# Six of sixteen pairs of row tiles of an MLP's first product by seven half-size products in place of eight, with the sums on GpSimd

## The chip, the cores and the metric

One core of one Trainium2 chip runs the whole kernel. The metric is the device time of one execution in microseconds; the time before is the median of three runs, 869.11 us (869.0 to 869.13). The engines have short names in the rows: PE is TensorE (PEld its weight loads), DVE is VectorE, ACT is ScalarE, POOL is GpSimd, SP is SyncE, which issues the DMA transfers. Each engine works through its own instructions in a fixed order.

## The reference

The kernel computes one decoder block in float32 on 512 tokens of width 1024: two attention-like branches, merged, then a squared-ReLU MLP, then gated embeddings. The change lies in the MLP:

```
x = x + merged @ w_out
h = rms_norm(x, mlp_norm_g)
x = x + jnp.square(jax.nn.relu(h @ w_ff1)) @ w_ff2      # w_ff1: 1024 x 4096, w_ff2: 4096 x 1024
gate = jax.nn.sigmoid(rms_norm(x, ple_norm_g) @ w_ple_gate)
x = x + gate * (p @ w_ple_proj)
return rms_norm(x, final_norm_g)
```

## The kernel before

**Products in three parts.** A float32 operand is split into a high part (`w_hi`, a copy rounded to fp32r, by ScalarE, line 175) and a low part (`w_lo`, the difference, by VectorE, line 176). A product of two split operands is three matmuls: high by high, high by low, low by high. `mm3` (lines 186 to 194) issues them with a weight tile of 128x128 as the stationary operand and the activations as the moving one; `rows3` (lines 201 to 209) has the activations stationary and the weights moving. `split` (line 220) does the same for activations.

**Weights.** All weights come as units of 128x1024 in the fixed order of the list `seq`. `load_to` issues the load of a unit into `w_raw` (two buffers), `fetch_to` makes its `w_hi` and `w_lo` (three buffers each), and `weights` hands it to the product. `fetch_to` runs two units ahead of the product, so the `w_hi` of a unit waits until TensorE is done with the unit three before it.

**The MLP in quarters.** The 4096 hidden rows are done in four quarters (`for qd`, lines 1216 to 1245). In each, the first product makes eight tiles of 128 hidden rows by 512 tokens (`m` from 0 to 7), each from one weight unit: 8 x 3 = 24 matmuls of 512 columns into one PSUM bank. `squared` (lines 1148 to 1167) takes max(0, .) times the norm's scale (`rs2`) on VectorE, squares on ScalarE, and builds the operands of the second product.

The second product is already done by seven block products in place of eight (Strassen in Winograd's form): the hidden rows 0 to 3 and 4 to 7 of the quarter and the two halves of the tokens are the blocks on one side, four weight blocks B11, B12, B21, B22 on the other. `seventh(qd, i, ...)` is one of the seven, of two weight units (p_ = 0 and 1) and 24 matmuls; `LEFT` lists its activation operand (`fA11`, `fA2`, `fS`, `fS3`), `RIGHT` its weight operand. The weight blocks are loaded into eight tiles of their own by `load_block`; the sums of them (T2, T1, T4 and B12 - B22) are made by VectorE (`sums_early`, `T1`, `T4`). `to_x` adds a finished result from PSUM to the residual `xs`.

**Order.** A scheduler places the instructions of every engine by their readiness in its own model; the program text gives the dependences, and `issue_after` adds a few by hand. GpSimd has no work in the MLP. The SBUF space is nearly full.

Of the kernel before, what the change touches and what calls it, by code (L numbers as in the profile page):

```python
# [18 lines left out]
P = 128  # L19
T = 512  # L20
# [20 lines left out]
U_PLE, U_QKV, U_RW, U_GSB, U_GRW, U_UPSB, U_UPRW, U_OUT, U_FF1, U_FF2, U_GATE = range(11)  # L41
UNITS = {U_PLE: 2, U_QKV: 12, U_RW: 14, U_GSB: 8, U_GRW: 8, U_UPSB: 4, U_UPRW: 4, U_OUT: 8, U_FF1: 32, U_FF2: 32, U_GATE: 8}
# [5 lines left out]
NUNITS = _n  # L48

# [36 lines left out]
def tile_block(ctx: ExitStack, tc: tile.TileContext, xT, xt, pT, wts, lora, cols_d, gfin_d, consts_d, out, dbg=None):  # L86
# [60 lines left out]
    ready, loaded = {}, []  # L147
# [3 lines left out]
    sources = {}  # L151

    def unit(i):
        return wts[UBASE[seq[i][0]] + seq[i][1]]

    def load_to(n):
        while len(loaded) < min(n, len(seq)):
            i = len(loaded)
            loaded.append(None)
            if seq[i][0] != U_FF2:  # L160
                loaded[i] = wpool.tile([P, 1024], F32, name="w_raw", bufs=2)
                sync.dma_start(out=loaded[i], in_=unit(i))

    def fetch_to(n, ahead=0):
        while state["i"] < min(n, len(seq)):
            i = state["i"]
            state["i"] += 1
            load_to(i + 1 + ahead)
            raw = loaded[i] if seq[i][0] != U_FF2 else sources[seq[i]]()
            if seq[i] in homes:  # L170
                hi, lo = homes[seq[i]]()
            else:
                hi = wpool.tile([P, 1024], F32R, name="w_hi")
                lo = wpool.tile([P, 1024], F32R, name="w_lo")
            act.copy(out=hi, in_=raw)  # L175
            dve.tensor_tensor(out=lo, in0=raw, in1=r32(hi), op=ALU.subtract)  # L176
            ready.setdefault(seq[i], []).append((hi, lo))

# [7 lines left out]
    def mm3(ps, w, base, rhs, k, first, last, t=slice(0, T)):  # L186
# [4 lines left out]
        pe.matmul(ps, wh, xh[:, k, t], start=first, stop=False)  # L191
        pe.matmul(ps, wh, xl[:, k, t], start=False, stop=False)  # L192
        pe.matmul(ps, wl, xh[:, k, t], start=False, stop=last)  # L193
        step()
# [82 lines left out]
    with ExitStack() as sA:  # L277
# [43 lines left out]
        with ExitStack() as s1:  # L321
# [18 lines left out]
            raws = [wpool.tile([P, 1024], F32, name="w_raw", bufs=2) for _ in range(2)]  # L340
# [719 lines left out]
    def norm_of(pool_, name):  # L1060

        st = pool_.tile([P, 3, TT], F32, name=name)
        sq = pool_.tile([P, D], F32, name="sqj", tag="T2a")
# [43 lines left out]
    fA11, fS3 = ([p4.tile([P, 4, HT], F32R, name=f"{n}{i}") for i in range(2)] for n in ("fA11", "fS3"))  # L1107
# [6 lines left out]
    LEFT = (fA11, part(fA2, 0), part(fS, 1), part(fS, 0), fS3, part(fS, 2), part(fA2, 1))  # L1114
# [4 lines left out]
    def kept(tt):  # L1119
        t = p4.tile([P, 512], F32, name="pl", tag="rk", bufs=4)  # L1120
        return t
# [7 lines left out]
    r2 = norm_of(p4, "st2")  # L1129

    def spread():

        ps = ps_main()
        for tt in range(TT):
            dg = p4.tile([P, P], F32, name="dg", bufs=2)
            dve.tensor_scalar(out=dg, in0=ident, scalar1=r2[:, tt:tt + 1], scalar2=float(D), op0=ALU.mult, op1=ALU.mult)
            pe.matmul(ps[:, tt * P:(tt + 1) * P], onesd, dg, start=True, stop=True)
        act.copy(out=rs2, in_=ps)
# [7 lines left out]
    lower = {}  # L1146

    def squared(ps, m):
        if m < 4:
            r = lower[m] = p4.tile([P, T], F32, name="rk", bufs=4)  # L1150
        else:
            r = p4.tile([P, T], F32, name="r")
# [3 lines left out]
        lo_, hi_ = r[:, 0:HT], r[:, HT:T]  # L1156
        if m < 4:
            split(fA11[0][:, m], fA11[1][:, m], lo_)
            minus(sums[:, 0], lo_, hi_)
            split(fS3[0][:, m], fS3[1][:, m], sums[:, 0])  # L1160
        else:
            k, low = m - 4, lower[m - 4]
            split(fA2[0][:, k], fA2[1][:, k], r.rearrange("p (j t) -> p j t", j=2))
            plus(sums[:, 1], low[:, HT:T], hi_)
            minus(sums[:, 2], sums[:, 1], low[:, 0:HT])
            minus(sums[:, 3], lo_, sums[:, 2])
            split(fS[0][:, k], fS[1][:, k], sums[:, 1:4])
# [3 lines left out]
    def load_block(qd, n, p_):  # L1171

        i = {"B11": 0, "B21": 2, "B12": 4, "B22": 6}[n] + p_
        t = blocks[n, p_] = p4.tile([P, 1024], F32, name=f"{n}{'ab'[p_]}")
        sync.dma_start(out=t, in_=wts[UBASE[U_FF2] + qd * 8 + i])

    def sums_early(p_):

        minus(blocks["B12", p_], blocks["B22", p_], blocks["B12", p_])
        blocks["T2", p_] = p4.tile([P, 1024], F32, name=f"T2{'ab'[p_]}")  # L1180
        plus(blocks["T2", p_], blocks["B12", p_], blocks["B11", p_])

    def T1(p_):
        minus(blocks["B11", p_], blocks["B22", p_], blocks["T2", p_])

    def T4(p_):
        minus(blocks["B21", p_], blocks["B21", p_], blocks["T2", p_])

    RIGHT = ("B11", "B21", "T2", "B11", "B12", "B22", "B21")
    BEFORE = {4: lambda: T1(0), 5: lambda: T1(1), 7: lambda: T4(0), 8: lambda: T4(1)}  # L1190
    for qd in range(4):
        for i in range(7):
            for p_ in range(2):
                def source(i=i, p_=p_):
                    BEFORE.get(2 * i + p_, lambda: None)()
                    return blocks[RIGHT[i], p_]
                sources[U_FF2, qd, i, p_] = source
    LOADS = [[("B12", 0), ("B22", 0)], [("B11", 0), ("B12", 1)], [("B22", 1), ("B11", 1)], [("B21", 0), ("B21", 1)]]
# [16 lines left out]

    for qd in range(4):
        waiting = []
        for m in range(8):
            w = weights(U_FF1, qd * 8 + m)
            for l in LOADS[m] if m < 4 else ():  # L1220
                load_block(qd, l[0], l[1])
            ps = ps_main()
            product(ps, w, hx)
            waiting.append((ps, m))
            if qd == 0 and m < 2:
                continue
            if qd == 0 and m == 2:
                spread()
            while waiting:
                squared(*waiting.pop(0))  # L1230
            if m in (2, 4):
                sums_early(m // 2 - 1)
# [12 lines left out]
        to_x(V, 1, 0)  # L1245

# [179 lines left out]
```

## Time and profile before

| what | value |
|---|---|
| median of the runs | 869.11 us |
| the profiled execution | 869.75 us, of which its span 867.7 us |
| granted TensorE clock, mean | 0.998 |
| everything ahead of the MLP's first product | 0 to about 480 us |
| the MLP's four quarters | 480 to 806.9 us |
| embeddings, gate, final norm, output | 806.9 to 867.7 us |

The second, third and fourth quarter start at 562.07, 643.67 and 725.27 us (the first matmul of each), and each takes 81.6 us. In the rows that follow, a line of a group gives line, engine, operation, output and inputs by the names of the program, shapes and count, then busy time and the mean of one in ns, then the idle time just ahead of them and who ended it. A line of a timeline gives start, duration, engine, line, operation and tiles. A line of windows gives start:end, the length, then busy time and count of PE, PEld, DVE, ACT and POOL, the granted clock, the DMA engines' share and GB/s.

### The profile page before, as it was taken

The page shows a single profiled execution, that of the slowest core. Times are in us where ns is not written, and L with a number is a line of the kernel's source. Part 1 is how long each engine was busy: PE and PEld are TensorE (multiplying, and loading weights), DVE is VectorE, ACT ScalarE, POOL GpSimd, SP SyncE. Part 2 cuts the span into 40 slices and gives each one's busy share as a digit, 9 for nine tenths or more (in the row PEclk, how much of TensorE's full clock was granted, in tenths as well). Part 3 has the DMA queues.
Part 4 walks back from the last instruction along what each step waited for, and adds up shares of the span by engine and source line. Part 5 has one row for each costly group of instructions (what it writes and reads, how often), then busy time and mean ns, then how long its engine had stood idle before and what let it go on. Part 6 is the DMA issues. An engine that isn't in the chain of part 4 may idle for free.

```text
span 867.7 us, 13424 instructions
## 1 busy us (share of the span) xinstructions
PE 851.4 (98%) x5182; PEld 686.8 (79%) x5182; DVE 678.1 (78%) x1228; ACT 448.6 (52%) x703; POOL 80.4 (9%) x138
## 2 busy tenths in 40 slices
PE   8999999999999999999999999999999999999996
PEld 5778787877777777777888888888888888888885
DVE  7899987896979888776754789858985987697767
ACT  6888887744335343534424464344434543453744
POOL 1432431002302111020000000000000000000000
PEclk9999999999999999999999999999999999999999
DMA  7212212221121224437935621531252034300422
GB/s 269 98 49 66 82 62 85 74 97 51 62 87 57 80 73 153 141 116 258 318 121 181 232 73 38 182 120 49 83 184 98 25 127 164 98 1 0 170 73 98
DMA packets 32272, 95.32 MB, mean 110 GB/s; under 512 B 3664, under 2 KB 3664, under 8 KB 32208
## 3 DMA queue, kind: packets, MB, share of 16 engines
q1 hardware_dynamic: 32208, 94.46, 32.6%
q8 instruction: 41, 0.67, 0.3%
q14 instruction: 23, 0.19, 0.1%
HBM read 83.96 MB, written 10.49 MB: 109 GB/s over the span
## 4 chain that ended last, share of the span: by engine, by line
PE 81%; DVE 10%; ACT 4%; issue 1%; DMA 1%; SPq 0%; POOL 0%; POOLq 0%; DVEq 0%; ACTq 0%
PE ps_m L191 13%; PE ps_m L193 13%; PE ps_m L192 13%; PE ps_m L206 9%; PE ps_m L207 9%; PE ps_m L208 9%; DVE w_lo L176 2%; PE ps_g L817 1%; PE ps_o L497 1%; PE ps_g L193 1%; PE ps_c L935 1%; PE ps_s L944 1%; PE ps_g L191 1%; PE ps_g L192 1%; PE ps_g L906 1%
## 5 line engine op out<-in xcount | busy, mean ns | idle before, releaser
L175 ACT CAST w_hi<-w_raw 128x1024 fp32r<-128x1024 f32 x94 | 99.0, 1053 | 170.4 <-PE ps_m L192 110.8
L176 DVE TENSOR_TENSOR w_lo<-w_raw,w_hi 128x1024 fp32r<-128x1024 f32 x94 | 115.1, 1225 | 37.6 <-ACT w_hi L175 37.2
L191 PE MATMUL ps_m<-h_hi,w_hi 128*128 128x512 f32 x320 | 130.6, 410 | 0.9 <-ACT h_hi L353 0.9
L192 PE MATMUL ps_m<-h_lo,w_hi 128*128 128x512 f32 x320 | 128.0, 400 | 0.0
L193 PE MATMUL ps_m<-h_hi,w_lo 128*128 128x512 f32 x320 | 127.5, 399 | 0.0
L191 PE MATMUL ps_m<-hx,w_hi 128*128 128x512 f32 x256 | 99.6, 390 | 0.4 <-ACT hx L1049 0.4
L192 PE MATMUL ps_m<-hx,w_hi 128*128 128x512 f32 x256 | 99.6, 390 | 0.0
L193 PE MATMUL ps_m<-hx,w_lo 128*128 128x512 f32 x256 | 99.5, 389 | 0.0
L191 PEld LDWEIGHTS ps_m<-h_hi,w_hi 128*128 128x128 f32 x320 | 60.7, 190 | 11.4 <-ACT h_hi L353 1.6
L193 PEld LDWEIGHTS ps_m<-h_hi,w_lo 128*128 128x128 f32 x320 | 60.3, 188 | 11.8
L192 PEld LDWEIGHTS ps_m<-h_lo,w_hi 128*128 128x128 f32 x320 | 60.5, 189 | 11.0 <-DVE h_lo L354 1.1
L191 PEld LDWEIGHTS ps_m<-hx,w_hi 128*128 128x128 f32 x256 | 48.0, 188 | 10.5 <-ACT hx L1049 0.6
L192 PEld LDWEIGHTS ps_m<-hx,w_hi 128*128 128x128 f32 x256 | 48.1, 188 | 10.2 <-DVE hx L1050 0.2
L193 PEld LDWEIGHTS ps_m<-hx,w_lo 128*128 128x128 f32 x256 | 48.0, 188 | 10.0
L207 PE MATMUL ps_m<-w_lo,fS 128*128 128x512 f32 x128 | 49.8, 389 | 0.0
L208 PE MATMUL ps_m<-w_hi,fS 128*128 128x512 f32 x128 | 49.8, 389 | 0.0
L206 PE MATMUL ps_m<-w_hi,fS 128*128 128x512 f32 x128 | 49.8, 389 | 0.0
L1291 POOL TENSOR_SCALAR r<-s 128x1 f32<-128x1 f32 x1 | 0.5, 519 | 478.9 <-DVE t L1271 478.9
L208 PE MATMUL ps_m<-w_hi,fA 128*128 128x512 f32 x96 | 37.4, 389 | 0.0
L207 PE MATMUL ps_m<-w_lo,fA 128*128 128x512 f32 x96 | 37.3, 389 | 0.0
L206 PE MATMUL ps_m<-w_hi,fA 128*128 128x512 f32 x96 | 37.3, 389 | 0.0
L221 ACT CAST fS<-sums 128x256 fp32r<-128x256 f32 (+1 forms) x32 | 19.8, 620 | 33.3 <-DVE sums L1141 33.3
(378 smaller groups left out, 1911.6 us busy)
## 6 DMA issues: line engine op xcount, KB each, us to landing
w_raw<-in_wts_dram SPq DMA_DIRECT2D x98, 512.0 KB, 3.5
gates<-gg SPq DMA_DIRECT2D x16, 256.0 KB, 2.1
x_in<-in_xT_dram SPq DMA_DIRECT2D x8, 256.0 KB, 5.7
tmp<-gates SPq DMA_DIRECT2D x8, 256.0 KB, 4.0
upsb<-tmp SPq DMA_DIRECT2D x8, 256.0 KB, 3.5
ga<-upsb SPq DMA_DIRECT2D x8, 256.0 KB, 5.4
gb<-gates SPq DMA_DIRECT2D x8, 256.0 KB, 5.4
xs<-in_xt_dram SPq DMA_DIRECT2D x4, 512.0 KB, 5.9
```

The source lines that it names most:

```text
L175: act.copy(out=hi, in_=raw)
L176: dve.tensor_tensor(out=lo, in0=raw, in1=r32(hi), op=ALU.subtract)
L191: pe.matmul(ps, wh, xh[:, k, t], start=first, stop=False)
L192: pe.matmul(ps, wh, xl[:, k, t], start=False, stop=False)
L193: pe.matmul(ps, wl, xh[:, k, t], start=False, stop=last)
L206: pe.matmul(ps, xh[:, k + j], wh, start=first and j == 0, stop=False, skip_group_check=True)
L207: pe.matmul(ps, xh[:, k + j], wl, start=False, stop=False, skip_group_check=True)
L208: pe.matmul(ps, xl[:, k + j], wh, start=False, stop=last and j == 1, skip_group_check=True)
L221: act.copy(out=hi, in_=src)
L497: pe.matmul(ps_o[:, j * P:T], vv[:, j, hh, :, :].rearrange("p a d -> p (a d)"), part[:, ZB[j]:ZB[j] + ZN[j]], start=j == 2 and part is wh, ...
L817: last = pe.matmul(ps[rows, k], left[rows, k, :], rhs[rows, k], start=True, stop=True)
L906: pe.matmul(ps[:, j * P:(j + 1) * P], Z[:, hh * 4 + g * 2 + cp, :], MA[:, g * 4 + j, :], start=True, stop=True)
```

## The change

For six pairs of row tiles, the pairs (quarter, kp) in `SEVEN`, the first product too is done by seven products of halves. A pair is the two row tiles kp and kp + 4 of a quarter, blocks on one side; the two halves of the 1024 inputs and the two halves of the tokens are the other divisions. The seven products have 4 x 3 matmuls of 256 columns each. The other ten pairs stay at two units of 24 matmuls of 512 columns (`eight`), but the two tiles of a pair now follow each other.

For this the weights need four sums of 128x512 a pair (`four_sums`, by GpSimd): two of them form the unit S12, one overwrites half of the raw unit (S3), one is the half unit S4. GpSimd also makes the low parts of S12 and S4; ScalarE makes all high parts, and VectorE the low part of S3. The activations need four sums once (`right_sums`, by GpSimd, eight operations of 128x1024), split into `tb` by `right_parts`.

In PSUM some of the seven products add up in place; ScalarE copies four partial results out (`kept_`), VectorE adds them to later ones, and the max and scale then read SBUF instead of PSUM.

The blocks of the second product are no longer held: B11 becomes T2 and B12 becomes B12 - B22 in place (`early_sums`, now by GpSimd, at pairs 1 and 3), and B21 and B22 are streamed as units through `w_raw`, with the two T differences made in place by VectorE (`changed`). `w_raw` has four buffers in place of two. `operands` builds all operands of the second product for a pair at once, after its second tile; `fA11` takes the place of `pin`, which is loaded and split anew at the end of the MLP.

```
+PAIRS = (0, 1, 2, 3)
+SEVEN = {(1, 0), (1, 2), (2, 0), (2, 2), (3, 0), (3, 2)}
+EARLY = (1, 3)
+FF2_FROM = {0: 0, 1: 2, 3: 6, 5: 6, 6: 2}
...
-        seq += [(U_FF1, qd * 8 + m) for m in range(8)]
+        for kp in PAIRS:
+            if (qd, kp) in SEVEN:
+                seq += [(U_FF1, qd * 8 + kp), (U_S12, qd, kp), (U_S3, qd, kp), (U_S4, qd, kp)]
+            else:
+                seq += [(U_FF1, qd * 8 + kp), (U_FF1, qd * 8 + kp + 4)]
...
+    def four_sums(i):
+        load_to(i + 1)
+        a, b = loaded[i - 1], loaded[i]
+        x = sums12[seq[i][1:]] = sP4["pool"].tile([P, 3, 512], F32, name="s124")
+        pool.tensor_tensor(out=x[:, 0], in0=b[:, 0:512], in1=b[:, 512:1024], op=ALU.add)
+        pool.tensor_tensor(out=x[:, 1], in0=x[:, 0], in1=a[:, 0:512], op=ALU.subtract)
+        pool.tensor_tensor(out=b[:, 0:512], in0=a[:, 0:512], in1=b[:, 0:512], op=ALU.subtract)
+        pool.tensor_tensor(out=x[:, 2], in0=a[:, 512:1024], in1=x[:, 1], op=ALU.subtract)
...
             act.copy(out=hi, in_=raw)
-            dve.tensor_tensor(out=lo, in0=raw, in1=r32(hi), op=ALU.subtract)
+            if seq[i][0] in (U_S12, U_S4):
+                with tc.issue_after(state["lo"]) if seq[i][0] == U_S4 else nullcontext():
+                    state["lo"] = pool.tensor_tensor(out=lo, in0=raw, in1=r32(hi), op=ALU.subtract).ins
+            else:
+                dve.tensor_tensor(out=lo, in0=raw, in1=r32(hi), op=ALU.subtract)
...
+    def right_sums():
+        raw = {}
+        for n, k, t in (("11", 0, 0), ("12", 0, 1), ("22", 1, 1), ("21", 1, 0)):
...
+            pool.tensor_tensor(out=raw[n], in0=r32(b[0]), in1=r32(b[1]), op=ALU.add)
+        for n, to, x, y in ((0, "11", "12", "11"), (2, "12", "22", "12"), (1, "22", "22", "11"), (3, "21", "21", "22")):
+            pool.tensor_tensor(out=raw[to], in0=raw[x], in1=raw[y], op=ALU.subtract)
...
+    def operands(kp, r):
+        low, up = r
+        sums = const.tile([P, 4, HT], F32, name="sums", tag="lora_w")
+        split(fA11[0][:, kp], fA11[1][:, kp], low[:, 0:HT])
+        summed(sums[:, 0], low[:, 0:HT], low[:, HT:T], ALU.subtract)
+        split(fA2[0][:, kp], fA2[1][:, kp], up.rearrange("p (j t) -> p j t", j=2))
+        summed(sums[:, 1], low[:, HT:T], up[:, HT:T], ALU.add)
+        summed(sums[:, 2], sums[:, 1], low[:, 0:HT], ALU.subtract)
+        summed(sums[:, 3], up[:, 0:HT], sums[:, 2], ALU.subtract)
+        split(fS3[0][:, kp], fS3[1][:, kp], sums[:, 0])
+        split(fS[0][:, kp], fS[1][:, kp], sums[:, 1:4])
...
+    def block_product(ps, w, base, rhs, first):
+        for k in range(4):
+            mm3(ps, w, base, rhs, k, first and k == 0, k == 3, slice(0, HT), True)
...
+        X, Y, W, Z = (ps_main()[:, 0:HT] for _ in range(4))
+        w = weights(U_FF1, qd * 8 + kp)
+        block_product(X, w, 0, right(0, TA), True)
+        c1 = kept_(X, "c1")
+        block_product(Y, w, 512, right(1, TA), True)
+        dve.tensor_tensor(out=r[0][:, TA], in0=Y, in1=c1, op=ALU.add)
+        w = weights(U_S12, qd, kp)
+        block_product(W, w, 0, sums_(0), True)
+        c5 = kept_(W, "c5")
+        block_product(X, w, 512, sums_(1), False)
+        c2 = kept_(X, "c2")
+        w3 = weights(U_S3, qd, kp)
+        block_product(Z, w3, 512, sums_(3), True)
+        c4 = kept_(Z, "c4")
+        w = weights(U_S4, qd, kp)
+        block_product(W, w, 0, right(1, TB), False)
+        dve.tensor_tensor(out=r[0][:, TB], in0=W, in1=c2, op=ALU.add)
+        squared(0, r[0], r[0])
+        block_product(X, w3, 0, sums_(2), False)
+        dve.tensor_tensor(out=r[1][:, TA], in0=X, in1=c4, op=ALU.add)
+        dve.tensor_tensor(out=r[1][:, TB], in0=X, in1=c5, op=ALU.add)
+        squared(1, r[1], r[1])
+        operands(kp, r)
...
+        b11 = blocks["T2", p_] = p4.tile([P, 1024], F32, name=f"B11{'ab'[p_]}")
+        b12 = blocks["T3", p_] = p4.tile([P, 1024], F32, name=f"B12{'ab'[p_]}")
+        block("B12", 4, b12)
+        b22 = block("B22", 6, wpool.tile([P, 1024], F32, name="w_raw", bufs=4))
+        block("B11", 0, b11)
+        with tc.issue_after(state["lo"]) if "lo" in state else nullcontext():
+            summed(b12, b22, b12, ALU.subtract, pool)
+        summed(b11, b12, b11, ALU.add, pool)
...
+            for i in (3, 6):
+                changed[U_FF2, qd, i, p_] = lambda t, p_=p_: minus(t, t, blocks["T2", p_])
```

How the order moves is seen at three places; the numbers behind the names tell buffers apart. First ScalarE where the first quarter's second product ends and the second quarter's first product begins. Before, the two last weight units (B21a, B21b) are followed by the units of the next first product:

```order
L175 CAST w_hi_5659<-B21a_5261 128x1024
L175 CAST w_hi_5677<-B21b_5263 128x1024
L175 CAST w_hi_5697<-w_raw_5675 128x1024
L175 CAST w_hi_5715<-w_raw_5695 128x1024
L175 CAST w_hi_5740<-w_raw_5713 128x1024
```

Now (5692 and 5711 are the two last units, 5731 the next quarter's first unit, 5752 its S12, 5776 its S3, 5809 its S4):

```order
L219 CAST w_hi_5692<-w_raw_5669 128x1024
L219 CAST w_hi_5711<-w_raw_5689 128x1024
L219 CAST w_hi4_5809<-s124_5735 128x512
L219 CAST w_hi_5731<-w_raw_5708 128x1024
L219 CAST w_hi_5752<-s124_5735 128x1024
L219 CAST w_hi_5776<-w_raw_5729 128x1024
```

The high part of S4, which reads the last of the four sums, has come ahead of the high part of the quarter's first unit.

Second, VectorE where the second quarter's first product ends. Before (6039 and 6080 are the second and third weight unit of the second product, the `r` are tiles 5 to 7 of the quarter):

```order
L1153 SCALAR_TENSOR_TENSOR r_6017<-ps_m_5988,rs2_4975 128x512
L222 TENSOR_TENSOR fS1_4974<-sums_5980,fS0_4973 128x768
L176 TENSOR_TENSOR w_lo_6039<-B11b_5814,w_hi_6038 128x1024
L222 TENSOR_TENSOR fA21_4972<-r_6017,fA20_4971 128x512
L1144 TENSOR_TENSOR sums_6020<-rk_5847,r_6017 128x256
L1141 TENSOR_TENSOR B11b_5814<-B22b_5812,T2b_5946 128x1024
L1141 TENSOR_TENSOR sums_6020<-sums_6020,rk_5847 128x256
L1141 TENSOR_TENSOR sums_6020<-r_6017,sums_6020 128x256
L1153 SCALAR_TENSOR_TENSOR r_6057<-ps_m_6028,rs2_4975 128x512
L176 TENSOR_TENSOR w_lo_6080<-B21a_5859,w_hi_6079 128x1024
```

Now (6187 and 6238 are the second and third weight unit of the second product; 6289 and 6309 are raw units of its fourth block product):

```order
L225 TENSOR_TENSOR w_lo_6187<-w_raw_6153,w_hi_6186 128x1024
L273 TENSOR_TENSOR fS1_4977<-sums_6122,fS0_4976 128x768
L273 TENSOR_TENSOR fA11_5115<-r_6205,fA11_5115 128x256
L1224 TENSOR_TENSOR sums_6211<-r_6205 128x256
L1218 TENSOR_TENSOR w_raw_6289<-w_raw_6289,B11a_5902 128x1024
L273 TENSOR_TENSOR fS31_4973<-sums_6211,fS30_4972 128x256
L1218 TENSOR_TENSOR w_raw_6309<-w_raw_6309,B11b_6135 128x1024
L1228 SCALAR_TENSOR_TENSOR r_6206<-ps_m_6174,rs2_4978 128x512
L225 TENSOR_TENSOR w_lo_6238<-w_raw_6184,w_hi_6237 128x1024
```

The two differences with B11a and B11b (T2, which GpSimd now makes) stand ahead of the low part of the third weight unit, and all operands of the last pair are built here.

Third, GpSimd in the second quarter, where it had nothing before:

```order
L1224 TENSOR_TENSOR B12a_5903<-w_raw_5905,B12a_5903 128x1024
L1224 TENSOR_TENSOR B11a_5902<-B12a_5903,B11a_5902 128x1024
L186 TENSOR_TENSOR s124_5926<-w_raw_5920 128x512
L187 TENSOR_TENSOR s124_5926<-s124_5926,w_raw_5861 128x512
L188 TENSOR_TENSOR w_raw_5920<-w_raw_5861,w_raw_5920 128x512
L189 TENSOR_TENSOR s124_5926<-w_raw_5861,s124_5926 128x512
L223 TENSOR_TENSOR w_lo_5957<-s124_5926,w_hi_5956 128x1024
L223 TENSOR_TENSOR w_lo4_6043<-s124_5926,w_hi4_6042 128x512
L1224 TENSOR_TENSOR B12b_6136<-w_raw_6138,B12b_6136 128x1024
L1224 TENSOR_TENSOR B11b_6135<-B12b_6136,B11b_6135 128x1024
```

These ten, after the six of the quarter's first pair, are one chain in a fixed order: the early sums of half a, the second pair's four sums and two low parts, the early sums of half b.

More of the change, by code (lines that the diff above doesn't have):

```diff
@@ L1155, in squared @@
         sums = const.tile([P, 4, HT], F32, name="sums", tag="lora_w")
[L1156 to L1167, printed above, removed]
@@ L1169, in tile_block @@
-    blocks = {}
[L1171 to L1184, printed above, removed]
@@ L1245, in tile_block @@
         to_x(V, 1, 0)
+    pins = pr.tile([P, 2, 2, T], F32R, name="pins2", tag="o_rw")
+    for j in range(2):
+        t = p4.tile([P, T], F32, name="praw2", tag="r", bufs=2)
+        sync.dma_start(out=t, in_=pT[:, j])
+        split(pins[:, 0, j], pins[:, 1, j], t)
+    pin = [pins[:, i] for i in range(2)]
     sM.close()
```

151 lines of the change are left out of this document (104 added, 47 removed).

## The prediction

> **What bounds the kernel now.** I read the page first (busy shares, chain), then the stretches of one MLP quarter, then the timelines of single engines.
>
> ```profile
> PE 851.4 (98%) x5182; PEld 686.8 (79%) x5182; DVE 678.1 (78%) x1228; ACT 448.6 (52%) x703; POOL 80.4 (9%) x138
> PE 81%; DVE 10%; ACT 4%; issue 1%; DMA 1%; SPq 0%; POOL 0%; POOLq 0%; DVEq 0%; ACTq 0%
> L191 PE MATMUL ps_m<-hx,w_hi 128*128 128x512 f32 x256 | 99.6, 390 | 0.4 <-ACT hx L1049 0.4
> 562.10:605.60 43.50, 43.50 (x194) 36.02 (x193) 29.41 (x46) 18.95 (x29) 0.00 (x0) 1.00 0.26 86
> 605.60:643.70 38.10, 38.10 (x170) 31.55 (x169) 34.21 (x40) 17.39 (x18) 0.00 (x0) 1.00 0.38 124
> ```
>
> The chain is TensorE. In the last two rows (start:end, length, then busy PE, PEld, DVE, ACT, POOL, the granted clock) the first product of the second quarter takes 43.5 us and the second 38.1: a quarter is 81.6 us, TensorE is never idle in it, and GpSimd does nothing at all. VectorE is busy 63.6 of the 81.6 us. So two questions decide: how much TensorE time goes, and whether the engines that feed it keep up.
>
> **What TensorE saves.** All matmuls here carry one weight load each. Their spacing, from the timeline:
>
> ```profile
> 502.01 0.39 PE L193 MATMUL ps_m<-hx,w_lo 128*128 128x512 f32 x1
> 523.77 0.39 PE L193 MATMUL ps_m<-hx,w_lo 128*128 128x512 f32 x1
> 854.05 0.28 PE L206 MATMUL ps_m<-wg,hx 128*128 128x256 f32 x1
> 859.68 0.28 PE L208 MATMUL ps_m<-wg,hx 128*128 128x256 f32 x1
> ```
>
> Between the first two rows lie four units of 24 matmuls: 21.76 / 96 = 0.2267 us for 512 columns. The last two are the first and last of 48 in a row (three lines, x16 each): 5.63 / 47 = 0.1198 us for 256 columns. A pair by eight is 48 x 0.2267 = 10.88 us. By seven it is 7 x 4 x 3 = 84 matmuls of 256 columns, 84 x 0.1198 = 10.06. That is 0.82 us a pair, **4.9 us for six pairs**. An eighth of the arithmetic is 1.36 us a pair, but a half-width matmul costs 53% of a full one. Everything else must stay hidden for this to be the result.
>
> **What GpSimd takes on, and what that does to VectorE.** GpSimd's only two-input operations before stand in the attention stage:
>
> ```profile
> L480 POOL TENSOR_TENSOR sums_lo<-sums,sums_hi x8: 735/741/1257, 40.3 to 127.9; 128x256 fp32r<-128x256 f32 x8
> 77.19 0.74 POOL L480 TENSOR_TENSOR sums_lo<-sums,sums_hi 128x256 fp32r<-128x256 f32 x1
> 77.28 1.19 DVE L410 TENSOR_TENSOR kk<-kT,kk 64x512 fp32r<-64x512 f32 x1
> 104.18 0.68 DVE L410 TENSOR_TENSOR kk<-kT,kk 64x512 fp32r<-64x512 f32 x1
> 88.41 0.68 DVE L222 TENSOR_TENSOR spl<-sp,sph 128x512 fp32r<-128x512 f32 x1
> 88.44 1.26 POOL L480 TENSOR_TENSOR sums_lo<-sums,sums_hi 128x256 fp32r<-128x256 f32 x1
> 102.33 0.74 POOL L480 TENSOR_TENSOR sums_lo<-sums,sums_hi 128x256 fp32r<-128x256 f32 x1
> 102.51 1.64 DVE L176 TENSOR_TENSOR w_lo<-w_raw,w_hi 128x1024 fp32r<-128x1024 f32 x1
> 103.02 1.29 POOL L474 CAST sums_lo<-spl 128x128 fp32r<-128x128 f32 x1
> 62.38 0.69 DVE L394 SCALAR_TENSOR_TENSOR qT<-ps_m,rs 128x512 f32<-128x512 f32 x1 [0.34 <-PE ps_m L193]
> 62.38 0.74 POOL L480 TENSOR_TENSOR sums_lo<-sums,sums_hi 128x256 fp32r<-128x256 f32 x1
> ```
>
> This is the centre of the case. The two engines exclude each other. At 77.28 a VectorE subtraction starts inside a GpSimd one and takes 1.19 us where the same takes 0.68 alone: it stood for 0.51. At 102.51 the split w_lo takes 1.64 (mean of its kind 1.22). The other way round, the GpSimd operation at 88.44 meets a running VectorE one and takes 1.26 in place of 0.74. Only the pair at 62.38 overlaps freely: that VectorE operation reads one input from PSUM. So a VectorE operation with both inputs in SBUF waits for a running GpSimd one, and the reverse. A GpSimd operation of 256 columns holds VectorE off for about 0.55 us (102.51 less 0.13 of lead: 1.64 - 1.22 = 0.42, and 0.13 before), so 2.15 ns a column; by its whole 0.741 us it is 2.89 ns.
>
> The rule for this stands in the Trainium skill, "SBUF — State Buffer", section "Who interferes with whom": the later of the two "fully blocks" until the first has finished, the pair of ports being held for the whole instruction. The block is what the rows show; the whole length is not, since 0.51 to 0.55 of 0.74 us were lost. By the rule's wording the 2.15 below would be 2.89, and the sum some 20 us more (third rival).
>
> GpSimd's columns in a quarter with two pairs by seven: four sums of 512, one split of 1024 and one of 512 a pair, 3,584; with the early sums (four of 1024), 2 x 3,584 + 4,096 = 11,264, thus 24.2 us of exclusion a quarter, mostly inside the first product.
>
> **Does VectorE still keep up?** Its own pace, start to start, in the tight place of before:
>
> ```profile
> 602.96 0.69 DVE L222 TENSOR_TENSOR fA<-r,fA 128x512 fp32r<-128x512 f32 x1
> 603.56 0.42 DVE L1144 TENSOR_TENSOR sums<-rk,r 128x256 f32<-128x256 f32 x1
> 603.90 1.22 DVE L1141 TENSOR_TENSOR B11b<-B22b,T2b 128x1024 f32<-128x1024 f32 x1
> 612.54 1.28 DVE L1214 TENSOR_TENSOR xs<-ps_m,xs 128x512 f32<-128x512 f32 x2
> 613.74 0.95 DVE L222 TENSOR_TENSOR fS<-sums,fS 128x768 fp32r<-128x768 f32 x1
> 614.61 1.22 DVE L176 TENSOR_TENSOR w_lo<-T2a,w_hi 128x1024 fp32r<-128x1024 f32 x1
> 615.74 1.22 DVE L176 TENSOR_TENSOR w_lo<-T2b,w_hi 128x1024 fp32r<-128x1024 f32 x1
> 616.47 0.39 PE L206 MATMUL ps_m<-w_hi,fS 128*128 128x512 f32 x1
> ```
>
> A step of 512 columns is 0.60 us, of 256 0.34, of 768 0.87, of 1024 1.13. And w_lo of T2a, done at 615.83, is wanted by the second matmul after 616.47: less than 0.9 us in hand. VectorE is already at its edge where the second product begins.
>
> Take the window of a later quarter from its first matmul to the second matmul of the second product's third weight unit (the fA2 product, first half). TensorE needs 20.1 + 21.8 + 5.4 = **47.3 us** for it. Counted in the changed order, VectorE has to finish in it 11 w_lo and 2 block differences (13 x 1.13 = 14.7), 21 operations of 256 columns in SBUF (7.1), 7 of 512 (4.2), 3 of 768 (2.6), and from PSUM 4 of 512, 2 to_x and 8 additions of 256 (the last not in this trace: between 0.34 and 0.60, taken as the nearest, 0.34): 6.3. Together **34.9 us**. GpSimd has to finish all but the first pair's four sums (2,048 columns, which fit before the quarter): 9,216 x 2.15 = **19.8 us**, since the in-order VectorE queue holds the difference that reads B11b, GpSimd's last result, ahead of that w_lo. Of GpSimd's time at most the 6.3 us of PSUM work is free cover; I take half, 3. Near the start both engines also sit: VectorE has four w_lo in 9 us, and GpSimd waits until a weight buffer is free and loaded:
>
> ```profile
> w_raw<-in_wts_dram SPq DMA_DIRECT2D x98, 512.0 KB, 3.5
> 638.43 1.06 ACT L175 CAST w_hi<-w_raw 128x1024 fp32r<-128x1024 f32 x1 [1.67 <-PE ps_m L208]
> ```
>
> The buffer comes free with S3's w_lo about 4 us into the quarter, its load lands 3.5 us later: some 3 us in which neither can use the other's absence. 34.9 + 19.8 - 3 + 3 = 54.7 against 47.3: **TensorE waits 7.4 us in each of three quarters, 22 us.** Followed operation by operation, it falls in three places: about 1 us at the quarter's start (ScalarE now has S4's w_hi, which needs the fourth sum, ahead of the first unit's w_hi of 1.06 us), about 3 at S3's w_lo of the second pair, and 3 to 4 at the fA2 unit. Bounds a quarter: 34.9 + 19.8 - 6.3 = 48.4, 1 us late; without cover and at 2.89 ns, 34.9 + 26.6 + 3 = 64.5, 17 us late.
>
> **The rest.** The first quarter has no pair by seven, but right_sums (8 x 1024 columns, 17.6 us at 2.15) and four more splits of 1.13 on VectorE. By the same sum it ends between nothing and 6 us late; GpSimd starts while VectorE still has gaps, so I take 2. The rebuilt pin (two splits of 512) lies in the last second product, where VectorE has 3.9 of 38.1 us free: nothing, 1.2 us if that cover is gone. ScalarE gains four copies of 256 a pair; it is busy 19.0 of 43.5 us. DMA: the same weights, B22 and B21 read twice; its share is 0.26 to 0.38. More w_raw buffers also reorder instructions before the MLP; there the change may give or take 2 us, and I take nothing.
>
> Sum, on the profiled execution (867.7 us span, 869.75 in all): 869.75 - 4.9 + 22.2 + 2 = 889.05; that execution stands 0.64 above the median of the runs, so **888.4 us**.
>
> **Rivals.**
> 1. *Hidden after all, faster.* The blocked VectorE work is late but not too late. It needs GpSimd to cost VectorE under 47.3 - 34.9 = 12.4 of its 19.8 us, so 7.4 or more in the shadow of PSUM work and waits. For it: VectorE idles 14 of 43.5 us now, and buffers are three deep. Against: the in-order queues, and the 0.9 us in hand. Gives 869.1 - 4.9 = 864.2.
> 2. *Late a little.* 1 to 4 us a quarter, as with full PSUM cover: 867 to 877.
> 3. *Whole-length exclusion*, at 2.89 ns a column: 26.6 in place of 19.8, 14 us a quarter, about 909; with no cover at all 17 us, about 918.
> 4. *The pair by seven saves nothing.* If 84 narrow matmuls with alternating stationary tiles ran slower than 0.1295 us each, 10.88 us would be used up; the row gives 0.1198 in the same pattern, so this has hardly a chance of its own, and would add 5 us to any case.
>
> **How the numbers follow.** Forecast (4 to 12 us late a quarter, 878 to 903): 0.53. Rival 1: 0.22. Rival 2: 0.13. Rival 3: 0.12. A measurement of this kernel tells 0.2% (1.7 us) from no change. Faster takes rival 1 and a little of 2's lower edge: 0.23; within 0.2% (867.4 to 870.8) from 2: 0.05; slower the rest: 0.72. The range has to reach to rival 1's end and into rival 3: 864 to 908 leaves out about 0.15.
>
> **What would show it.** Spacing of the 256-column matmuls near 0.12 us. GpSimd's 1024-column operations at 2.3 us or more, and w_lo in the MLP well above its 1.22 us. A quarter of 80.0 us plus waits, near 87, with TensorE's idle time released by VectorE's w_lo, before the second pair's S3 products and the fA2 unit. Wrong I am if w_lo grows but TensorE does not wait (rival 1), if the first quarter carries the loss, or if the loss is before 480 us.

## The result: slower, and by twice what was forecast

| | before | after |
|---|---|---|
| median | 869.13 us (869.0 to 871.1, 5 runs) | 908.25 us (907.8 to 909.82, 5 runs) |
| profiled execution: its time, its span | 869.75, 867.7 us | 909.19, 907.4 us |
| ratio of the runs, 95% interval | | 1.045 (1.0434 to 1.0465) |

The forecast was 888.4 us, with a range up to 908. The direction came out as written, and so did the way in which GpSimd takes time from VectorE; the size, and the places where TensorE waits, did not. The page of the changed kernel, its busy line and its chain (shares of the span by engine):

```profile
PE 860.2 (95%) x5398; PEld 699.8 (77%) x5398; DVE 734.7 (81%) x1242; ACT 467.9 (52%) x745; POOL 207.1 (23%) x198
PE 51%; issue 17%; DVE 16%; POOL 6%; ACT 5%; DMA 5%; SPq 0%; POOLq 0%; DVEq 0%; ACTq 0%
```

TensorE held 81% of the chain before and holds 51% now; VectorE and GpSimd, 10% and nothing before, hold 22%. TensorE is busy longer although it has less to do, which the last section comes back to. Where the time went is read by quarters of the MLP. These are the stretches of the changed kernel from the first matmul of one quarter to that of the next (start:end, length, then busy time and count of PE, PEld, DVE, ACT, POOL, the granted clock, and the DMA share and GB/s), and behind them the same first quarter of the kernel before:

```profile
482.22:579.75 97.53, 88.76 (x369) 70.81 (x369) 84.41 (x105) 42.49 (x61) 33.55 (x15) 0.95 0.42 143
579.75:668.25 88.50, 82.38 (x432) 70.91 (x432) 75.50 (x89) 41.13 (x59) 32.20 (x16) 0.98 0.41 143
668.25:756.79 88.54, 82.41 (x433) 71.10 (x433) 75.49 (x89) 41.15 (x59) 32.29 (x16) 0.98 0.41 143
```

```profile
479.13:562.10 82.97, 82.97 (x369) 68.50 (x370) 70.74 (x109) 40.04 (x56) 0.00 (x0) 1.00 0.40 130
```

The spans of these two executions differ by 39.7 us: 3.1 before the first product starts (482.22 against 479.13), 14.6 in the first quarter (97.53 against 82.97), 6.9 in each of the next two (88.5 against 81.6), and the remaining 8.2 in the last quarter and behind it. The first quarter has no pair by seven, and yet it loses the most. What TensorE waited for from 470 to 860 us (us in total, times, longest), the first six rows:

```profile
PE ps_m L242 <- ACT c L1275: 13.6, 3, 4.5
PE ps_m L243 <- DVE hx L1101: 3.2, 1, 3.2
PE ps_m L242 <- ACT w_hi L219: 2.6, 3, 0.9
PE ps_m L258 <- DVE w_lo L225: 2.3, 2, 1.2
PE ps_m L244 <- DVE w_lo L225: 2.3, 3, 0.8
PE ps_m L257 <- ACT fA L272: 2.2, 1, 2.2
```

The greatest wait is named after ScalarE's copy c, three times 4.5 us, once in each of quarters 2 to 4. The timelines of VectorE and GpSimd ahead of the one at 610.85 show who is late (start, duration):

```profile
592.57 1.85 DVE L1224 TENSOR_TENSOR sums<-r 128x256 f32<-128x256 f32 x1
594.34 1.77 DVE L1228 SCALAR_TENSOR_TENSOR r<-r,rs 128x512 f32<-128x512 f32 x1
596.04 1.51 DVE L273 TENSOR_TENSOR fA<-r,fA 128x256 fp32r<-128x256 f32 x1
597.47 1.51 DVE L273 TENSOR_TENSOR fS<-sums,fS 128x256 fp32r<-128x256 f32 x1
598.90 2.31 DVE L225 TENSOR_TENSOR w_lo<-w_raw,w_hi 128x1024 fp32r<-128x1024 f32 x1
594.10 1.47 POOL L186 TENSOR_TENSOR s<-w_raw 128x512 f32<-128x512 f32 x1
595.65 1.62 POOL L187 TENSOR_TENSOR s<-s,w_raw 128x512 f32<-128x512 f32 x1
597.23 1.47 POOL L188 TENSOR_TENSOR w_raw<-w_raw 128x512 f32<-128x512 f32 x1
598.66 1.47 POOL L189 TENSOR_TENSOR s<-w_raw,s 128x512 f32<-128x512 f32 x1
```

The two engines take turns, one instruction each. A VectorE step of 256 columns, 0.41 us long before, takes 1.51: it waits until GpSimd's step of 512 columns is through. From end to end the VectorE steps follow each other by 1.69, 1.44, 1.43 and 2.23 us; less their own pace from the prediction (0.60, 0.34, 0.34, 1.13) that is 1.09, 1.10, 1.09, 1.10. One GpSimd step of 512 columns therefore takes **1.10 us of VectorE's time, 2.15 ns a column**, the very figure of the forecast. The 1.47 to 1.62 us of GpSimd's rows above contain its own wait for VectorE's step; where VectorE does nothing (574.3 to 579.7 us), such a step takes 1.28 us:

```profile
576.82 1.28 POOL L189 TENSOR_TENSOR s<-w_raw,s 128x512 f32<-128x512 f32 x1
```

Then the way to TensorE, ScalarE's rows and TensorE's:

```profile
607.75 0.40 ACT L272 CAST fS<-sums 128x256 fp32r<-128x256 f32 x1 [0.85 <-DVE sums L1224]
608.06 1.04 ACT L219 CAST w_hi<-w_raw 128x1024 fp32r<-128x1024 f32 x1
609.24 0.63 ACT L1229 ACTIVATE r<-r 128x512 f32<-128x512 f32 x1
609.91 0.62 ACT L272 CAST fA<-r 128x512 fp32r<-128x512 f32 x1
610.43 0.36 ACT L1275 COPY c<-ps_m 128x256 f32<-128x256 f32 x1
610.85 0.58 PE L242 MATMUL ps_m<-tb,w_hi 128*128 128x256 f32 x1 [4.52 <-ACT c L1275]
```

A pair by seven adds its second product onto the bank X, whose first content the copy c1 must have taken. c1 stands in ScalarE's queue behind the square and the splits of the pair before, and those wait for VectorE. For the most part ScalarE passes the lateness on; a w_hi of 1.04 us that stands in its queue there adds to it.

### The profile page after: what moved, and what is told of

The parts are those of the page before. It is cut to its first block, busy times and chain, and to the rows that moved or that the text cites. A ratio compares the mean times of both kernels' runs of the same rounds, so it can differ in the third digit from the quotient of the medians.

```text
span 907.4 us, 14112 instructions
## 1 busy us (share of the span) xinstructions
PE 860.2 (95%) x5398; PEld 699.8 (77%) x5398; DVE 734.7 (81%) x1242; ACT 467.9 (52%) x745; POOL 207.1 (23%) x198
## 4 chain that ended last, share of the span: by engine, by line
PE 51%; issue 17%; DVE 16%; POOL 6%; ACT 5%; DMA 5%; SPq 0%; POOLq 0%; DVEq 0%; ACTq 0%
PE ps_m L242 8%; PE ps_m L244 8%; PE ps_m L243 8%; PE ps_m L258 4%; PE ps_m L259 4%; PE ps_m L257 4%; DVE w_lo L225 3%; DMA w_raw<-in_wts_dram 2%; ACT w_hi L219 2%; DVE sums L1224 1%; DVE r L1228 1%; POOL B11b L1224 1%; POOL B12b L1224 1%; PE ps_z L556 1%; PE ps_o L548 1%
## 5 line engine op out<-in xcount | busy, mean ns | idle before, releaser
L219 ACT CAST w_hi<-w_raw 128x1024 fp32r<-128x1024 f32 x134 | 140.5, 1050 | 173.7 <-PE ps_m L243 91.7
L225 DVE TENSOR_TENSOR w_lo<-w_raw,w_hi 128x1024 fp32r<-128x1024 f32 x134 | 179.6, 1342 | 59.1 <-ACT w_hi L219 58.5
L242 PE MATMUL ps_m<-hx,w_hi 128*128 128x512 f32 (+1 forms) x232 | 84.0, 363 | 3.9 <-ACT w_hi L219 2.6
L243 PE MATMUL ps_m<-hx,w_hi 128*128 128x512 f32 (+1 forms) x232 | 84.2, 363 | 3.2 <-DVE hx L1101 3.2
L244 PE MATMUL ps_m<-hx,w_lo 128*128 128x512 f32 (+1 forms) x232 | 84.4, 364 | 2.3 <-DVE w_lo L225 2.3
L242 PEld LDWEIGHTS ps_m<-hx,w_hi 128*128 128x128 f32 x232 | 44.3, 191 | 11.6 <-ACT w_hi L219 3.8
L243 PEld LDWEIGHTS ps_m<-hx,w_hi 128*128 128x128 f32 x232 | 44.7, 193 | 10.1 <-DVE hx L1101 3.8
L244 PEld LDWEIGHTS ps_m<-hx,w_lo 128*128 128x128 f32 x232 | 44.5, 192 | 9.3 <-DVE w_lo L225 2.9
L242 PE MATMUL ps_m<-tb,w_hi 128*128 128x256 f32 x96 | 29.6, 308 | 13.6 <-ACT c L1275 13.6
L257 PE MATMUL ps_m<-w_hi,fA 128*128 128x512 f32 x96 | 38.4, 400 | 3.6 <-ACT fA L272 2.2
L1229 ACT ACTIVATE r<-r 128x512 f32<-128x512 f32 x32 | 19.8, 629 | 36.8 <-DVE r L1228 36.3
```

Source lines behind the costliest of these rows:

```text
L242: pe.matmul(ps, wh, xh[:, k, t], start=first, stop=False, skip_group_check=skip)
L243: pe.matmul(ps, wh, xl[:, k, t], start=False, stop=False, skip_group_check=skip)
L244: pe.matmul(ps, wl, xh[:, k, t], start=False, stop=last, skip_group_check=skip)
L257: pe.matmul(ps, xh[:, k + j], wh, start=first and j == 0, stop=False, skip_group_check=True)
```

## The experiments

Twelve kernels, each beside runs of the kernel before on the same chip; the ratios are against those (medians 869.67 to 870.12 us).

**All sums to VectorE (e1).**

```
-    pool.tensor_tensor(...)      four sums of a seven, lows of S12 and S4, right_sums
+    dve.tensor_tensor(...)
-            summed(b12, b22, b12, ALU.subtract, pool)
-        summed(b11, b12, b11, ALU.add, pool)
+            summed(b12, b22, b12, ALU.subtract, dve)
+        summed(b11, b12, b11, ALU.add, dve)
```

> All two-input sums that the change gave to GpSimd in the MLP (the weights' four sums, the low parts of S12 and S4, the early block sums, the activations' sums) are done by VectorE; nothing else changes. Theory (the two engines exclude each other, 2.15 ns of VectorE time lost per GpSimd column): VectorE does a column itself in 1.1 ns, so it gains about 10 us a quarter and the waits shrink a lot; 872 to 895 us. Rival (GpSimd's sums ran in VectorE's gaps and relieved it; the waits come from something else): VectorE gets 12 us more a quarter on top and the time rises, 920 us or more.

Measured: 874.23 us, 1.0045 (1.0029 to 1.0062): 34 us less than the change, by giving VectorE more to do. The second quarter of this run, columns as above:

```profile
570.00:650.20 80.20, 80.20 (x433) 69.70 (x432) 73.38 (x105) 42.20 (x58) 0.00 (x0) 1.00 0.48 158
```

VectorE does 16 instructions more than in the change's second quarter (105 against 89) and is busy 73.4 us instead of 75.5. The 32.2 us of work on GpSimd saved VectorE nothing; they cost it more than doing the work itself. TensorE is never idle here.

**Which of the sums (e7, e8, e10).** Each moves one part of e1 alone: the eight right sums; the sevens' sums and lows; the early sums of the second product (e10 also drops the `issue_after` ahead of these).

```
e7   right_sums:  -  pool.tensor_tensor(...)    +  dve.tensor_tensor(...)
e8   four_sums, lows of S12 and S4:  the same
e10  early_sums:  -  summed(..., pool)          +  summed(..., dve)
```

> Only the eight sums of right halves ahead of the first quarter go from GpSimd to VectorE; the sevens' sums and lows and the early sums of the second product stay on GpSimd. Theory (these eight instructions, 19 us of GpSimd, push VectorE's split of hx and its first work back, and that is most of the first quarter's loss of about 14 us): the split waits for less than 1 us at TensorE, the first quarter loses 4 to 6 us instead of 14, quarters 2 to 4 stay at 88.5 us each; 897 to 901 us. Rival (the first quarter's loss comes from the early sums of the second product on GpSimd, which stay): 905 us or more.

> Only the sevens' four sums and their two low parts go from GpSimd to VectorE; the sums of right halves and the early sums of the second product stay on GpSimd. Theory (exclusion in quarters 2 to 4 costs 8.2 us a quarter and three fifths of the GpSimd columns there are the sevens'): what is left of GpSimd's work costs little, since one quarter with the early sums alone on GpSimd and no sevens lost nothing; 883 to 887 us, the first quarter's 14 us unchanged. Rival (VectorE becomes full with 6 sums and lows more per pair beside the exclusion by the early sums): 892 to 900 us.

> Only the early sums of the second product (four of 1024 columns a quarter) go from GpSimd to VectorE; right sums and the sevens' work stay on GpSimd. Theory (VectorE and GpSimd share one time, and a column on GpSimd beside VectorE costs more of it than on VectorE: 4 x 3.0 us on GpSimd at 0.74 against 4 x 1.22 us, 4 us a quarter): 892 to 896 us. Rival (the early sums lie in the second product, where VectorE has slack, and the loss is the sevens' alone): 905 us or more.

Measured: e7 903.88 us, 1.0404 (1.038 to 1.0428); e8 892.85, 1.0267 (1.0252 to 1.0282); e10 897.8, 1.0323 (1.0308 to 1.0339). Against the change that is 4.4, 15.4 and 10.4 us, 30 in all of e1's 34, so the parts nearly add up. e7 and e8 missed the theory's numbers: the right sums alone give back 4 us and not 7 to 11, and e8 lies in its rival's range, since with the sevens' work on VectorE the early sums on GpSimd still cost. The waits of e8, first two rows:

```profile
PE ps_m L258 <- DVE w_lo L225: 6.0, 5, 1.4
PE ps_m L242 <- ACT c L1275: 4.6, 6, 1.7
```

The wait for the copy shrank from 4.5 us to 1.7 at most, and waits for w_lo at the second product took its place. No one group of GpSimd's work is harmless or the sole cause. e10 came 2 us above its theory: the early sums, which its rival held to lie in slack, are worth 10 us, half of it in the first quarter.

**The sevens away (e3, e11, e4, e5).** All run by eight pairs where a seven is dropped; streamed blocks, the order by pairs and the early sums on GpSimd stay.

```
-SEVEN = {(1, 0), (1, 2), (2, 0), (2, 2), (3, 0), (3, 2)}
e3   +SEVEN = set(), and no right_sums() and right_parts()
e11  +SEVEN = set()
e4   +SEVEN = {(1, 0), (2, 0), (3, 0)}
e5   +SEVEN = {(1, 2), (2, 2), (3, 2)}
```

> No pair by seven, and no activation sums (they would be unused); the streamed blocks, the order of tiles in pairs, the early sums on GpSimd and four w_raw buffers stay. Theory (the loss is the seven's sums, and in the first quarter the activation sums): close to before, 869 to 874 us, with the 2 to 3 us that the part ahead of the MLP has lost kept, and no waits of over 1 us at the start of a second product. Rival (operands of the last pair built late, and block differences behind GpSimd's early sums, cost at every second product's start as in the first quarter, 7 us): 869 + 2 + 4 x 7 = 899 us.

> No pair by seven, but the sums of right halves and their split are made as in the change (nothing uses them). Against the run without both (875.7 us). Theory (the first quarter's 14 us are the right sums' and their split's, on top of the 2 to 3 us that the streamed blocks cost there anyway): 886 to 888 us, all of the difference before the second quarter begins. Rival (they only cost so much where sevens follow, since the wait would otherwise be made up by the quarter after): 876 to 880 us.

> Sevens only in the first pair of quarters 2 to 4; the third pair by eight again. Theory A (each wait belongs to its pair: 2.0 us a quarter at the first, 6.1 us at the third with the slow matmuls behind its wait): 908.25 - 3 x (6.1 - 0.8) = 892 us. Theory B (the quarter's length is VectorE's and GpSimd's common time, which half of the sevens brings below TensorE's 81 us): no waits over 0.5 us in quarters 2 to 4; 908.25 - 3 x (8.2 - 0.8) = 886 us. Rival (the loss comes from the streamed blocks and the order, not from the sevens): 904 us or more.

> Sevens only in the third pair of quarters 2 to 4; the first pair by eight again. Theory A (each wait belongs to its pair): 908.25 - 3 x (2.0 - 0.8) = 904.7 us, and the wait for the copy of X stays at 4.5 us. Theory B (the common time of VectorE and GpSimd sets the quarter, and it is below TensorE's with one seven): 886 to 889 us, the wait for the copy under 1 us.

Measured: e3 875.74 us, 1.006 (1.0045 to 1.0075); e11 886.52, 1.0186 (1.0172 to 1.02); e4 891.19, 1.0247 (1.0221 to 1.0274); e5 896.61, 1.0307 (1.0291 to 1.0322). e11 less e3 is 10.8 us: **the right sums and their split cost this in the first quarter, with nothing using them.** Its waits, first three rows, are those of the change in that quarter:

```profile
PE ps_m L243 <- DVE hx L1101: 3.2, 1, 3.2
PE ps_m L257 <- ACT fA L272: 2.2, 1, 2.2
PE ps_m L257 <- ACT w_hi L219: 1.3, 1, 1.3
```

e3 lies 1.7 us above its theory's bound; it has a part ahead of the MLP that is 1.7 us longer and one wait of 2.5 us for w_lo in the second product of the first quarter, where its theory had none over 1 us. e4 came within 1 us of theory A, each wait belonging to its pair. e5 fell between the theories: the wait for the copy stayed, at 2.7 us instead of 4.5, so part of what the third pair pays is lateness that the first pair has left behind. Each seven costs, and the third pair's more (17 us by e4, where it is dropped) than the first's (12 by e5); both together are 22 us (the change less e11), less than the two added, so part of the loss is shared.

**Right sums later (e2).** Does a better place in the first quarter hide them?

```
+        gate = p4.tile([P, 1], F32, name="gate")
+        g = pool.tensor_copy(out=gate, in_=r2[:, 0:1])
-            pool.tensor_tensor(out=raw[n], ...)
+            with tc.issue_after(g.ins):
+                pool.tensor_tensor(out=raw[n], ...)
```

> GpSimd's eight activation sums in the first quarter start only when the norm's root is done (a one-column copy on GpSimd that reads it stands ahead of them), so that they cannot stand in the way of the last split of hx. Theory (in the first quarter 3.2 us of waiting and some 3 us of slower matmuls behind it come from VectorE's hx split and its tiny root steps being held by these sums): 902 to 904 us. Rival (the sums only move their blocking on to the operands, and the wait at the start of the second product, 7 us now, grows as much): 908 us.

Measured: 911.33 us, 1.0471 (1.0456 to 1.0487), 3 us beyond even the rival. The wait for the split of hx is gone, and this stands for it:

```profile
PE ps_m L1217 <- DVE dg L1216: 5.8, 3, 3.5
```

The sums now hold up the norm's broadcast (`dg`). This later place is no better than the first; others were not tried.

**TensorE kept busy (e6).** Behind the wait for the copy the matmuls ran at half speed (last section). Here 36 useless matmuls into a bank of their own stand ahead of X's second product in each quarter's third pair.

```
+        if kp == 2:
+            for _ in range(36):
+                pe.matmul(V_, w[0][:, 0:P], tb[0][:, 0, 0, :], start=True, stop=True, skip_group_check=True)
```

> 36 matmuls without use (256 columns, into a bank of their own) stand ahead of the second product on X in each second pair by seven, in the place where TensorE waits 4.7 us for the copy c1. Theory (after a wait of some us the matmuls run at about half speed for 2.7 us, since the clock granted falls): the wait stays, the slow stretch behind it goes, 3 x 1.3 = 4 us less, 904 us. Rival (the slow spacing has another cause, such as operands that arrive late): unchanged, 908 us, and the spacing behind the wait still 0.21 us.

Measured: 907.57 us, 1.043 (1.0412 to 1.0448), no gain that counts. The same second quarter, and the place of the wait:

```profile
578.01:666.47 88.46, 85.61 (x469) 73.97 (x469) 75.77 (x89) 41.00 (x59) 32.20 (x16) 1.00 0.44 143
604.43 4.48 PE L1291 MATMUL ps_m<-tb,w_hi 128*128 128x256 f32 x36
609.12 0.39 PE L242 MATMUL ps_m<-tb,w_hi 128*128 128x256 f32 x1 [0.21 <-ACT c L1275]
609.35 0.28 PE L243 MATMUL ps_m<-tb,w_hi 128*128 128x256 f32 x1
```

The clock is full, the slow stretch is gone, and the quarter takes 88.46 us as against 88.50: what was gained there, about 1.2 us, is mostly waited for at a later w_lo (1.0 us). So the length of the quarter is set by VectorE with GpSimd, and TensorE's slow matmuls lay in its shadow.

**A version without GpSimd, and the part ahead of the MLP (e9, e12).** e1 still lost 2.4 us ahead of the MLP and some small waits in its first quarter. e9 starts from e1, lets the split of the right sums run as soon as they exist, and names the four raw weight buffers as two names of two. e12 takes those two extra buffers, and the pair w_hi4 and w_lo4, from the MLP's own pool.

```
e9   -  with tc.issue_after(state["rs2"].ins):       (and state["dg"].ins)
     -  wpool.tile([P, 1024], F32, name="w_raw", bufs=4)
     +  wpool.tile([P, 1024], F32, name="w_rawb" if both and turn["n"] % 2 else "w_raw", bufs=2)
e12  +  sP4["pool"].tile([P, 1024], F32, name="w_rawb", bufs=2)
     +  sP4["pool"].tile([P, 512], F32R, name="w_hi4", bufs=1)      (and w_lo4)
```

> All sums and lows on VectorE as in the run of 874.2 us; besides, the four raw weight buffers are two names of two, of which the part ahead of the MLP uses one as before the change, and the split of the right sums no longer waits for the norm's broadcast. Theory (2.4 us lost ahead of the MLP are the order that four buffers under one name give there; the small waits of the first quarter are VectorE's work piled up behind the norm): 868 to 871 us, first product of the MLP within 0.5 us of 479.1. Rival (the front is the same, VectorE is full anyway): 873 to 875 us.

> As the run of 870.31 us (all sums and lows on VectorE, right sums' split early), but the two extra raw weight buffers and the fourth operand's pair lie in the MLP's own pool instead of the weights' pool, so that the part ahead of the MLP has the addresses that it had before the change. Theory (what is lost ahead of the MLP comes from where the longer weights' pool puts the tiles of that part, by which its instructions wait for other tiles and stand in another order): its order is that of before, the first product of the MLP starts within 0.6 us of 479.1 instead of at 482.2, and 866.5 to 868.5 us. Rival (the shift comes from the added work right ahead of the first product): 870 us, first product at 481 or later.

Measured: e9 870.31 us, 1.0003 (0.9994 to 1.0012); e12 868.49, 0.9983 (0.9973 to 0.9992). The first product of the MLP in e9, then in e12:

```profile
482.23 0.73 PE L248 MATMUL ps_m<-hx,w_hi 128*128 128x512 f32 x2 [1.29 <-ACT hx L1106]
```

```profile
479.17 0.73 PE L250 MATMUL ps_m<-hx,w_hi 128*128 128x512 f32 x2 [0.40 <-ACT hx L1108]
```

e9's rearrangement removed the first quarter's small waits but one of 0.6 us, and nothing ahead of it. e12 differs from e9 only in which pool those buffers come from (and so in which of them the prefetch uses; the gate's units use the first two alone), and its first product starts at 479.17, as before the change (479.13). TensorE's instructions ahead of the MLP also stand in the order of before again. The change also sets `dynamic_dma_scratch_size=2048`; e12 keeps that, so it is not what moved this part. So what is lost ahead of the MLP is not added work: it comes with the longer weights' pool. Its size is less sure than the two rows suggest. The change and the ten other kernels with its weights' pool (all but e9 and e12) start their first product between 480.43 us (e8) and 482.43 us (e11), one execution each, thus 1.3 to 3.3 us late; and the medians of e9 and e12 differ by 1.8 us. That this works through the addresses that the earlier stages' tiles get is the likeliest reading; which tiles then wait for which was not followed. e12 is the only version faster than the kernel before, by 0.17% (0.08 to 0.27), about the limit of what such a measurement tells; a quarter of the 4.9 us that TensorE saves.

## Why the prediction was right and where it was wrong

- **TensorE's saving: right.** The 256-column matmuls of the sevens follow each other by 0.120 us (in e6 from 609.35 to 611.98, 22 steps in 2.63 us), the figure of the forecast, and with all sums on VectorE a later quarter has no wait of note. The 4.9 us are there; e12 shows how little of them is left when all else is nearly hidden.
- **Exclusion at 2.15 ns a column: right,** by the 1.10 us a step of 512 columns above. (The prediction's own working of it is less firm: the lead of 0.13 us at 102.51 is not in its rows, where GpSimd's step starts 0.18 us ahead.) e1 shows that the sums on GpSimd are the cause of 34 us. That they act by the time that VectorE loses, and not by GpSimd's own slower steps, is read from VectorE's stretched steps and from the waits, of which ScalarE and VectorE end all; at the start of quarters 2 to 4, 2.6 us in all, ScalarE itself had waited for GpSimd's fourth sum, and there no run parts the two. The third rival, exclusion over the whole length of an instruction, gave 909 and so nearly the measured time, but for a wrong reason: its 2.89 ns come from a step of 256 columns and would make one of 512 cost 1.48 us, when the whole step is 1.28 long. The rule of the Trainium skill, "SBUF — State Buffer", section "Who interferes with whom", that the later one is blocked until the first is through, agrees in kind; what is lost is 1.10 of the 1.28 us and not quite the whole.
- **Quarters 2 to 4: right in kind, short in size.** "TensorE waits 7.4 us in each of three quarters, 22 us": it is 88.5 less 80.0, thus 8.5 us, 26 in three. e6 confirms the way of the sum (common time of VectorE and GpSimd against TensorE's), since filling TensorE's wait changes nothing. The places were partly wrong. About 2 us fall at the quarter's start as forecast (1 was said), but the greatest wait is not at S3's w_lo or the fA2 unit. It is at the copy c1 in the third pair: the working followed VectorE's results to TensorE and overlooked that X is written twice, with a copy between in ScalarE's queue.
- **The first quarter: the step that failed.** "By the same sum it ends between nothing and 6 us late; GpSimd starts while VectorE still has gaps, so I take 2." It is 14.6 us, of which the right sums and their split are 10.8 (e11 less e3). The sum counted GpSimd's 17.6 us against gaps of VectorE in the whole quarter, and it does not list the four early sums, which this quarter has too (4 x 1024 columns, 8.8 us at 2.15). The eight right sums run at its very start, beside a chain of tiny steps on VectorE:

```profile
487.06 2.38 POOL L1195 TENSOR_TENSOR x<-x,x 128x1024 f32<-128x1024 f32 x1
494.13 7.32 POOL L1195 TENSOR_TENSOR x<-x,x 128x1024 f32<-128x1024 f32 x3
487.25 2.22 DVE L291 TENSOR_SCALAR st<-st 128x4 int32<-128x4 int32 x1
491.13 0.48 DVE L1101 SCALAR_TENSOR_TENSOR hx<-ps_m,cols,hx 128x256 fp32r<-128x256 f32 x1
491.66 0.79 PE L243 MATMUL ps_m<-hx,w_hi 128*128 128x512 f32 x1 [3.19 <-DVE hx L1101]
496.75 2.23 DVE L295 SCALAR_TENSOR_TENSOR st<-st 128x4 f32<-128x4 f32 x1
```

  These steps of the norm's root have four columns and take 0.16 us alone. With GpSimd's 1024 columns in between, several take 2.2, and VectorE gets little done for 10 us. The last piece of hx's split stands behind the first of them, and TensorE waits 3.2 us for it. Most of the rest of the loss comes at 536 to 545 us: the early sums, on GpSimd from 518 to 530.5 us, hold VectorE up once more, and it cannot catch up before the second product. The first quarter of e7 (right sums on VectorE), of e10 (early sums on VectorE) and of e1 (both, and the sevens' work):

```profile
480.72:573.27 92.55, 87.09 (x368) 69.21 (x369) 80.37 (x112) 42.48 (x61) 17.09 (x8) 0.96 0.45 151
481.57:573.93 92.36, 87.18 (x369) 68.83 (x370) 83.34 (x110) 41.73 (x59) 21.81 (x11) 0.98 0.45 151
481.54:570.00 88.46, 85.78 (x368) 67.62 (x369) 80.56 (x121) 43.37 (x61) 0.00 (x0) 1.00 0.47 158
```

  Against 97.53 the right sums' place is worth 5.0 us, the early sums' 5.2, and both 9.1. The other 5.5 us over the quarter of before (82.97) are there without any work on GpSimd: VectorE's added sums and splits, and what follows from them (e9, whose split runs earlier, has 2.8).
- **Ahead of the MLP: wrong,** "there the change may give or take 2 us, and I take nothing": 3.1 us in this execution (1.3 to 3.3 over the kernels with this pool), which go when the weights' pool has its old size (e12).
- **The rest:** the rebuilt pin at nothing holds, as far as the 8.2 us of the last quarter and behind (6.9 as in the others, and a wait of 1.1 us for w_lo at 829.6) leave nothing for it. "Wrong I am if the first quarter carries the loss": it carries more than a third of it.

The forecast for the profiled execution was 889.05 us and it took 909.19, 20.1 more. The first quarter has 12.6 of them (14.6 less 2), the part ahead 3.1, the three other quarters 3.4 (25.6 less 22.2), the wait at 829.6 the last 1.1.

## What to carry to other kernels

An idle GpSimd is no free engine beside a busy VectorE: for every two-input step in SBUF ask what it takes from VectorE, here 2.15 ns a column against the 1.10 ns a column that VectorE needs to do the step itself (1.13 us for 1024 columns). Count that in the stretch where the step runs and not over a whole stage: in a chain of tiny steps beside long GpSimd instructions a step can wait for a whole one of these, as four of them did here. And a change of a pool's size reaches code that it doesn't touch, so compare the order of the earlier stages before weighing the change itself.

## What the runs showed of the hardware that was not expected

Behind its longer waits TensorE ran at half its clock for a while. The stretches around the wait at 610.85, the one behind the wait for hx in the first quarter, and the one around the wait of 2.23 us at 542.51, with the granted clock in the third column from the end:

```profile
606.00:611.00 5.00, 0.48 (x4) 0.28 (x3) 4.53 (x8) 3.94 (x8) 0.23 (x1) 0.93 0.01 2
611.00:613.60 2.60, 2.60 (x13) 2.60 (x14) 2.57 (x6) 1.85 (x3) 0.00 (x0) 0.50 0.55 202
613.60:618.00 4.40, 4.40 (x38) 4.40 (x38) 4.15 (x4) 1.69 (x3) 3.91 (x2) 0.99 0.40 135
488.00:497.50 9.50, 6.31 (x17) 4.63 (x16) 9.23 (x12) 1.04 (x1) 7.11 (x4) 0.65 0.16 57
540.00:545.00 5.00, 2.77 (x8) 1.80 (x7) 5.00 (x8) 4.37 (x8) 0.00 (x0) 0.70 0.30 105
```

For 2.6 us after the wait of 4.52 us the clock is 0.50 and 13 matmuls of 256 columns take 0.21 us each instead of 0.12, a loss of about 1.2 us; after the wait of 3.19 us in the first quarter some 13 of 512 columns take 0.43 us instead of 0.23, about 2.6. After the wait of 2.23 us the spacing is 0.43 us too, until 545.3; just ahead of it TensorE had been busy only 1.50 of 4 us (536 to 540). This also makes TensorE's busy time grow. The Trainium skill, "TensorE: Matmul & The Clock Gate", section "What's actually happening", names a halved clock after an idle window of about 3.4 us; the trace agrees with the half, and shows it after waits of 3.19 and 2.23 us too. In quarters 2 to 4 it cost nothing that shows in e6's time; in the first it was not tried apart.
